# A two-layer convolution and attention trunk in split fp32: the second embedding's place, the query plan of the attention loop, softmax sums, squares and a bias

## The chip, the cores and the metric

The kernel runs on one core of a Trainium2 chip. A core has the engines TensorE (PE; matrix products, with PEld for its weight loads), VectorE (DVE), ScalarE (ACT), GpSimd (POOL) and SyncE (SP, which issues most transfers), an on-chip memory SBUF, and PSUM banks in which TensorE leaves its products. Transfers run on 16 DMA engines. The metric is device microseconds of one execution; less is better.

## The reference, cut to what matters

The input is one sequence of 1024 tokens of width 1024, all in fp32. There are two layers. They differ in the mixer; what stands behind it is the same:

```python
# layer 0: causal Conformer convolution
h = x @ w_in + b_in;  a, gate = split(h);  h = a * sigmoid(gate)
h = depthwise_conv(h, w_dw, 31 taps, causal) + b_dw
y = silu(layer_norm(h)) @ w_out + b_out
# layer 1: attention over the last 128 positions; 16 query heads, 4 key/value heads of 64
k, v = rope(x @ w_k), x @ w_v                       # 16 of the 64 dimensions are rotated
scores = where(0 <= qpos - kpos < 128, q @ k.T / 8, -inf)
lse = logaddexp(logsumexp(scores), sink)            # one sink per head
y = (exp(scores - lse) @ v) @ w_o
# both layers i
x = layer_norm(ALPHA * x + y)                       # ALPHA = 4 ** 0.25
x = layer_norm(ALPHA * x + square(relu(x @ w_up)) @ w_down)     # width 4096
x = x + (p[i] @ w_proj) * sigmoid(x @ w_gate)       # p[i]: 1024 x 256
```

The product `p[i] @ w_proj` depends on nothing that the layer computes. It is called the embedding here.

## The kernel before

**Arithmetic.** TensorE multiplies fp32 numbers in a rounded form (fp32r). So each operand is kept as a high part and a low part (the rest), and each product is three matmuls: high x high, high x low, low x high (`mm3`). In the names, `wh` and `wl` are the parts of a weight tile of 128 x 1024, and `xTh` and `xTl` those of the transposed tokens. ScalarE makes the high part by a copy with rounding ("CAST"), and VectorE the low part by a subtraction. A matmul is 128 x 128 weights against up to 512 columns.

**Order.** No engine's program is written out by hand. `Recorder` records every operation in program order; `schedule` is a list scheduler that then places them on the engines by the durations in `cost` and by priority, which is the place in program order plus what `later(by)` adds. It also hands out buffers: each tag (`SLOTS`) has a number of buffers, and an operation waits for a free one. `nc.move(a, b)` makes a buffer of one tag one of another. `nc.after(mark)` lets an operation wait for another one. Since all instructions are issued from one place, they all carry one line: L455 before the change, L467 after it. They are told apart by buffer names, such as ps (PSUM bank), z, g, t (128 x 512 in SBUF), E, X, A, B (larger tiles). `Stream` (`ws`) feeds weights through five slots: a transfer into `raw`, the cast to `wh`, the subtraction to `wl`.

**Stages around the change.**

*Convolution* (`conv`, to about 260 us). `conv_in` makes the gated input of one channel block in four parts, and `taps` does the 31 taps of a block as matmuls, after a trip of the block through HBM (`scr`). The two run interleaved, the taps five steps (LAG) behind, so that the last steps of the loop `for n in range(32 + LAG)` are taps alone. Then come: the embedding of layer 0 (`embed(0, (0, 1), "g")`, 16 output tiles of 6 matmuls, each copied by ScalarE into a buffer g and stored to HBM); the layer norm and SiLU of the convolution in four pairs of token tiles (`conv_ln`); loads of the residual x into the tiles E (tokens 0 to 3) and B (4 to 7), to each half of which VectorE adds the bias `bo`, not before `marks[3]`, the last pair of `conv_ln`; and `mix_out`, the output projection, whose PSUM result VectorE adds to these tiles, followed by a layer norm with a scaling on GpSimd.

*MLP* (`mlp(i)`). 32 blocks of 128 hidden channels. The first `HEAD[i]` (4 in layer 0, 6 in layer 1) and the last two are computed plainly. The others go in pairs with seven products of half size in place of eight, for which `token_forms` must first combine the tokens on VectorE. `square` is the activation, on every PSUM result:

```python
nc.scalar.activation(r, src, AF.Relu)
sq = r if src.buf.space == "PSUM" else src
nc.vector.scalar_tensor_tensor(out=sq, in0=src, scalar=0.0, in1=r, op0=ALU.max, op1=ALU.mult)
```

*Attention* (`attention`, the loop from 1181.9 to 1394.6 us). Keys, the first queries and two value tiles come first. The loop then goes over two pairs of key heads (`gp`) and eight token tiles (`n`); each step has, for two key heads, the `scores` of four query heads (matmuls, ScalarE's copy, VectorE's masked copy, its negated maximum, four exponentials on ScalarE, VectorE's sum and reciprocal, four scalings on GpSimd) and, one step later, the products with the `values`. Beside them TensorE gets filler through `beside(gp, n)`: in the first pair the second token half of the first queries (n = 0 to 2), six value tiles, the later queries (`rest(1, ...)`, n = 3 to 5, both halves) and at n = 7 the embedding of layer 1 through buffers B; in the second pair the output projection's weights at n = 1 and its first two pairs of tiles at n = 2 and 4. The queries go to HBM (qdh, qdl) and come back for the scores into X. Behind the loop stands the rest of the output projection.

Of the kernel before, what the change touches and what calls it, by code (L numbers as in the profile page):

```python
# [16 lines left out]
P = 128  # L17
# [3 lines left out]
NT = T // P  # L21
# [38 lines left out]
HEAD, TAIL = (4, 6), 2  # L60
# [3 lines left out]
WARM = 7  # L64
CST = 256 + NT * 32 + 2 * NH
# [122 lines left out]
class Recorder:  # L188
# [90 lines left out]
    def cost(self, o, outs, allv):  # L279
# [6 lines left out]
        if n == "dma_start":  # L286
            return 380.0
# [19 lines left out]
    def schedule(self):  # L307
# [11 lines left out]
        def both(o):  # L319
            if o.eng == "gpsimd":  # L320
                return o.name != "memset" and o.outv[0].n > 8
# [166 lines left out]
class Emit:  # L488
# [179 lines left out]
    def conv(self):  # L668
# [155 lines left out]
        outs = (x for c in range(8) for x in taps(c))  # L824
        for n in range(32 + LAG):
            next(ins, None)
            if n >= LAG:
                next(outs, None)
        for g in (ins, outs):
            assert next(g, LAG) == LAG  # L830
# [5 lines left out]
        with nc.later(EMBED_BY):  # L836
            self.embed(0, (0, 1), "g")
# [16 lines left out]
    def embed(self, i, cols, tag):  # L854

# [4 lines left out]
        for q, w in zip(cols, wk):  # L860
            for t in range(NT):
# [9 lines left out]
                nc.sync.dma_start(self.proj[i][t][:, q * HT : (q + 1) * HT], sb)  # L871
        ws.done(len(us))
# [146 lines left out]
    def mlp(self, i):  # L1019
# [9 lines left out]
        us = ws.get(4)  # L1029
# [3 lines left out]
        ws.done(4)  # L1033
# [374 lines left out]
    def attention(self):  # L1408
# [12 lines left out]
        ws.add(*[unit[k] for k in range(2, 8)])  # L1421
        us = ws.get(4)
# [26 lines left out]
        for t in range(2):  # L1449
            value_rows(t)  # L1450
# [5 lines left out]
        def beside(gp, n):  # L1456
            if gp == 0:
                if n < 3:
                    rest(0, n, (1,))
                if n % 2 == 0 and n < 6:  # L1460
                    value_rows(n + 2)
                    value_rows(n + 3)
                    if n == 4:
                        ws.done(2)
                if 3 <= n < 6:
                    rest(1, n - 3, (0, 1))
# [3 lines left out]
                return  # L1470
            if n == 1:
                ws.add(*[d["w_o"][0, u] for u in range(4)])
                self.ou = ws.get(4)
            if n in (2, 4):
                self.out_tiles(0, PAIRS[n // 2 - 1], self.ou)
# [50 lines left out]
    def scores(self, n, g, q, keys):  # L1526
# [220 lines left out]
```

## Time and profile before

| | |
|---|---|
| median of three runs | 2173.28 us (2170.75 to 2178.07) |
| the profiled execution's own time | 2170.38 us |
| its span in the trace | 2168.7 us |
| mean granted TensorE clock | 0.998 |
| instructions of TensorE / VectorE / ScalarE / GpSimd | 10187 / 2480 / 1555 / 432 |
| moved by DMA | 341.52 MB, 157 GB/s over the span |

How to read what follows. A *window* row gives, for a stretch from:to in us, the length, and then for TensorE, its weight loads, VectorE, ScalarE and GpSimd the busy time with the number of instructions; the last three are the granted clock, the busy share of the DMA engines and GB/s. For TensorE the sum of its durations is cut to what it covers, since matmuls are pipelined; a matmul's own duration is longer than the time from its start to the next one's start. A *wait* row reads "engine out <- who released it: us in all, count, longest". A *timeline* row has start, duration, engine, operation, out<-in with sizes, and in brackets the idle time before it and what ended that. A *group* row has the operation with its count, then busy us, mean ns of one, and idle time before with its releaser. A *transfer* row has the count, the KB of each and the median us from issue to landing.

### The profile page before, as it was taken

How to read it: one execution, taken by the hardware profiler on the slowest of the kernel's cores; microseconds unless marked ns; L12 is line 12 of the kernel's file. 1: busy time of each engine (PE TensorE's matmuls, PEld its weight loads, DVE VectorE, ACT ScalarE, POOL GpSimd, SP SyncE). 2: the span in 40 equal slices, each digit the busy share in tenths (PEclk: the TensorE clock that was granted, in tenths of full speed). 3: DMA queues.
4: the chain of work that ended last, by engine and by line, in shares of the span. 5: the costliest groups of instructions: out<-in, count | busy, mean ns of one | idle time of the engine just before them, and what ended most of it. 6: DMA issues, size and time to landing. Idle time of an engine off the chain costs nothing.

```text
span 2168.7 us, 28684 instructions
## 1 busy us (share of the span) xinstructions
PE 2147.9 (99%) x10187; PEld 1788.7 (82%) x10187; DVE 1649.9 (76%) x2480; ACT 893.3 (41%) x1555; POOL 252.6 (12%) x432
## 2 busy tenths in 40 slices
PE   9999999999999999999999999999999999999999
PEld 7888888888888888888888887788888888888887
DVE  7667686987777977889555777899677688878983
ACT  5233342444444333353333666543344433333441
POOL 0000042200000000003101444450000000000040
PEclk9999999999999999999999999999999999999999
DMA  7443632334447755541448689232444596455322
GB/s 230 119 115 87 187 126 81 119 130 157 155 152 268 256 174 175 175 131 36 152 134 227 186 240 269 89 126 78 148 154 160 169 333 206 140 171 177 95 68 102
DMA packets 193360, 341.52 MB, mean 157 GB/s; under 512 B 19392, under 2 KB 88512, under 8 KB 193216
## 3 DMA queue, kind: packets, MB, share of 16 engines
q1 hardware_dynamic: 191920, 338.90, 48.8%
q8 instruction: 80, 1.31, 0.2%
q10 hardware_dynamic: 1296, 0.79, 0.1%
q14 instruction: 64, 0.52, 0.1%
HBM read 235.80 MB, written 103.81 MB: 157 GB/s over the span
## 4 chain that ended last, share of the span: by engine, by line
PE 44%; DVE 3%; DMA 3%; SPq 1%; ACT 1%; issue 1%; POOL 0%; DVEq 0%; ACTq 0%; POOLq 0%
PE ps L455 31%; PE tr L455 13%; SPq L455 1%; DVE xTl L455 1%; DVE A L455 1%; DVE wl L455 0%; DMA B<-xsp 0%; ACT z L455 0%; DVE B L455 0%; DVE sm L455 0%; DMA qdh<-A 0%; DVE t L455 0%; DMA X<-qdh 0%; DMA adl<-t 0%; DMA A<-xsp 0%
## 5 line engine op out<-in xcount | busy, mean ns | idle before, releaser
L455 PE MATMUL ps<-xTl,wh 128*128 128x512 f32 x752 | 295.0, 393 | 0.1
L455 PE MATMUL ps<-xTh,wl 128*128 128x512 f32 x752 | 294.3, 392 | 0.0
L455 PE MATMUL ps<-xTh,wh 128*128 128x512 f32 x752 | 293.0, 391 | 0.2 <-ACT xTh L455 0.2
L455 PE MATMUL ps<-xTl,xTh 128*128 128x512 f32 x636 | 247.4, 389 | 0.0
L455 PE MATMUL ps<-xTh,xTl 128*128 128x512 f32 x636 | 247.4, 389 | 0.0
L455 PE MATMUL ps<-xTh 128*128 128x512 f32 x636 | 247.4, 389 | 0.0
L455 ACT CAST wh<-raw 128x1024 fp32r<-128x1024 f32 (+2 forms) x141 | 132.2, 940 | 245.4 <-PE ps L455 114.7
L455 DVE TENSOR_TENSOR wl<-raw,wh 128x1024 fp32r<-128x1024 f32 (+2 forms) x141 | 156.3, 1109 | 95.0 <-ACT wh L455 93.6
L455 POOL TENSOR_SCALAR sm<-sm 128x1 f32<-128x1 f32 x40 | 14.5, 363 | 1322.2 <-DVE sm L455 1320.7
L455 PEld LDWEIGHTS ps<-xTh,wh 128*128 128x128 f32 x752 | 141.2, 188 | 29.9 <-ACT xTh L455 0.9
L455 PEld LDWEIGHTS ps<-xTh,wl 128*128 128x128 f32 x752 | 141.4, 188 | 28.6
L455 PEld LDWEIGHTS ps<-xTl,wh 128*128 128x128 f32 x752 | 141.2, 188 | 28.3 <-DVE xTl L455 1.0
L455 PE MATMUL ps<-wh,xTh 128*128 128x512 f32 (+1 forms) x408 | 156.8, 384 | 0.3 <-ACT xTh L455 0.3
L455 PE MATMUL ps<-wl,xTh 128*128 128x512 f32 (+1 forms) x408 | 156.6, 384 | 0.0
L455 PE MATMUL ps<-wh,xTl 128*128 128x512 f32 (+1 forms) x408 | 156.5, 384 | 0.0
L455 PEld LDWEIGHTS ps<-xTl,xTh 128*128 128x128 f32 x636 | 119.4, 188 | 24.9
L455 PEld LDWEIGHTS ps<-xTh 128*128 128x128 f32 x636 | 119.4, 188 | 24.7
L455 PEld LDWEIGHTS ps<-xTh,xTl 128*128 128x128 f32 x636 | 119.3, 188 | 24.8
L455 ACT CAST xTh<-wh 128x1024 fp32r<-128x1024 f32 x74 | 77.6, 1049 | 122.6 <-PE ps L455 56.4
L455 ACT CAST wh<-g 128x512 fp32r<-128x512 f32 x100 | 59.8, 620 | 152.3 <-PE ps L455 80.6
L455 DVE TENSOR_TENSOR wl<-g,wh 128x512 fp32r<-128x512 f32 x100 | 66.3, 685 | 72.8 <-ACT wh L455 72.8
L455 DVE TENSOR_TENSOR E<-cst,g 128x1152 fp32r<-128x1152 f32 x64 | 86.1, 1352 | 43.5 <-PE ps L455 42.6
(294 smaller groups left out, 4891.3 us busy)
## 6 DMA issues: line engine op xcount, KB each, us to landing
wh<-hid SPq DMA_DIRECT2D x76, 512.0 KB, 4.0
raw<-in_w_up_dram SPq DMA_DIRECT2D x64, 512.0 KB, 3.5
wl<-in_w_down_dram SPq DMA_DIRECT2D x64, 512.0 KB, 4.6
hid<-zz SPq DMA_DIRECT2D x84, 256.0 KB, 2.9
hid<-t SPq DMA_DIRECT2D x78, 256.0 KB, 2.1
raw<-hid SPq DMA_DIRECT2D x34, 512.0 KB, 3.6
B<-scr SPq DMA_DIRECT2D x32, 256.0 KB, 4.1
t<-proj SPq DMA_DIRECT2D x32, 256.0 KB, 3.4
```

The source lines that it names most:

```text
L455: getattr(getattr(nc, o.eng), o.name)(*a, **k)
```

## The change

It has seven parts.

1. `HEAD` becomes (4, 4): in the second MLP two blocks fewer are computed plainly and one pair more by seven products.
2. The first ten output tiles of layer 0's embedding (two per step, `EARLY`) are emitted in the last five steps of the taps loop, through buffers z; the other six follow behind the loop as before.
3. The bias is added to the residual's tiles by 16 accumulating transfers that GpSimd issues, behind the same mark, in place of 16 VectorE additions.
4. `square` takes ScalarE's Square of the Relu result, in place of VectorE's instruction.
5. `beside` follows a table, `PLAN`. The second token half of the later queries moves into the second pair of key heads (n = 0 to 2; their weights are loaded a second time), two value tiles more stand ahead of the loop and the other four go in pairs to n = 1 and 3, and the output projection's weights and its two pairs of tiles move to n = 3, 3 and 5.
6. The embedding of layer 1 moves out of the loop, behind the first half of the output projection, through buffers t.
7. The sums of the exponentials come from `accum_out` of ScalarE's activations; VectorE's sum goes.

The scheduler's cost of a GpSimd transfer is set to 880 with it. By the programs' order TensorE has 10175 matmuls in place of 10187; VectorE 32 sums and 128 squares fewer; ScalarE 128 activations, 7 casts and 3 copies more; GpSimd 16 transfers more; SyncE 1190 transfers in place of 1187.

```diff
-HEAD, TAIL = (4, 6), 2
+HEAD, TAIL = (4, 4), 2
+EARLY = 2
+PLAN = (
+    {
+        0: [("query", 0, 0, (1,))], 1: [("query", 0, 1, (1,)), ("value", 4), ("value", 5)], 2: [("query", 0, 2, (1,))],
+        3: [("value", 6), ("value", 7)], 4: [("query", 1, 0, (0,))], 5: [("query", 1, 1, (0,))],
+        6: [("query", 1, 2, (0,)), ("load",)],
+    },
+    {
+        0: [("query", 1, 0, (1,))], 1: [("query", 1, 1, (1,))], 2: [("query", 1, 2, (1,))],
+        3: [("weight",), ("out", 0)], 5: [("out", 1)],
+    },
+)
...
+        early = self.embed_tiles(0, (0, 1), "z")
         for n in range(32 + LAG):
             next(ins, None)
             if n >= LAG:
                 next(outs, None)
+            if n >= 32:
+                with nc.later(EMBED_BY):
+                    for k in range(EARLY):
+                        next(early)
...
         with nc.later(EMBED_BY):
-            self.embed(0, (0, 1), "g")
+            for k in early:
+                pass
...
                 with nc.after(marks[MARK[t // 4]]):
-                    nc.vector.tensor_tensor(out=xt[q], in0=xt[q], in1=bo[q], op=ALU.add)
+                    nc.gpsimd.dma_start(xt[q], bo[q], accum_op=ALU.add)
...
         sq = r if src.buf.space == "PSUM" else src
-        nc.vector.scalar_tensor_tensor(out=sq, in0=src, scalar=0.0, in1=r, op0=ALU.max, op1=ALU.mult)
+        nc.scalar.activation(sq, r, AF.Square)
...
         ws.add(*[unit[k] for k in range(2, 8)])
+        ws.add(*[unit[k] for k in range(5, 8)])
...
-        for t in range(2):
+        for t in range(4):
             value_rows(t)
...
         def beside(gp, n):
+            for what, *k in PLAN[gp].get(n, ()):
+                if what == "query":
+                    rest(*k)
+                elif what == "value":
+                    value_rows(*k)
+                    if k[0] == NT - 1:
                         ws.done(2)
-                if n == 7:
-                    self.embed(1, (0, 1), "B")
+                elif what == "load":
                     self.load_residual(range(0, 4))
+                elif what == "weight":
+                    ws.add(*[d["w_o"][0, u] for u in range(4)])
+                    self.ou = ws.get(4)
+                else:
+                    self.out_tiles(0, PAIRS[k[0]], self.ou)
...
         for g in PAIRS[2:]:
             self.out_tiles(0, g, self.ou, last=g is PAIRS[-1])
+        self.embed(1, (0, 1), "t")
...
         for h in range(4):
-            nc.scalar.activation(s[:, h, 0 : P + 1], s[:, h, 0 : P + 1], AF.Exp, bias=nm[:, h : h + 1], scale=1.0)
-        nc.vector.tensor_reduce(out=su, in_=s[:, :, 0 : P + 1], axis=AXIS, op=ALU.add)
+            nc.scalar.activation(s[:, h, 0 : P + 1], s[:, h, 0 : P + 1], AF.Exp, bias=nm[:, h : h + 1], scale=1.0,
+                                 accum_out=su[:, h : h + 1])
```

Here is ScalarE's queue where the convolution ends, before: behind the last four of its transfers to scr come the taps' sums for the transposes (g<-ps with 64x256, the constants cst as bias), the first copy of the embedding (g3_586<-ps0_581) and the copies of the convolution's output into A.

```order
L455 ACTIVATE g3_545_2440<-ps0_546_2450,cst_261_325 64x256
L455 ACTIVATE g3_545_2440<-ps1_548_2479,cst_261_325 64x256 x2
L455 COPY g3_586_2728<-ps0_581_2696 128x512
L455 COPY A1_15_79<-tr1_551_2499 128x64
L455 COPY A3_17_81<-tr1_551_2499 128x64
L455 COPY A5_19_83<-tr1_551_2499 128x64
L455 ACTIVATE g2_562_2582<-ps3_557_2550,cst_261_325 64x256 x2
```

The same place after the change:

```order
L467 ACTIVATE g3_545_2440<-ps0_546_2450,cst_261_325 64x256
L467 COPY z0_49_113<-ps3_557_2550 128x512
L467 ACTIVATE g3_545_2440<-ps1_548_2479,cst_261_325 64x256 x2
L467 COPY z1_50_114<-ps2_561_2577 128x512
L467 COPY z2_51_115<-ps3_581_2703 128x512
L467 COPY z3_52_116<-ps0_582_2706 128x512
L467 COPY A1_15_79<-tr1_551_2499 128x64
```

Four tiles of the embedding (z0 to z3) are copied where one was; the first two were computed in banks 3 and 2, while the banks of the taps' sums are 0 and 1.

GpSimd's queue behind the last scaling of the convolution's layer norm (A7 by the factors in sm6), before: it goes on with the small steps of the first layer norm behind the output projection.

```order
L455 TENSOR_SCALAR A7_21_85<-A7_21_85,sm6_631_2979 128x512
L455 TENSOR_SCALAR sm15_639_3013<-sm9_634_2990 128x1
L455 TENSOR_TENSOR sm15_639_3013<-sm15_639_3013,mhalf_263_327 128x1
L455 TENSOR_SCALAR sm1_644_3030<-sm2_643_3028 128x1
L455 TENSOR_TENSOR sm1_644_3030<-sm1_644_3030,mhalf_263_327 128x1
```

After the change, 16 transfers stand between that scaling and those small steps, first the two halves of E0, then of E1, E2 and E3, then B0 to B7; the last four of them and what follows:

```order
L467 DMA B4_597_2785<-bo0_43_107 128x512
L467 DMA B5_600_2813<-bo1_44_108 128x512
L467 DMA B6_606_2844<-bo0_43_107 128x512
L467 DMA B7_611_2881<-bo1_44_108 128x512
L467 TENSOR_SCALAR sm15_638_3027<-sm9_636_3010 128x1
L467 TENSOR_TENSOR sm15_638_3027<-sm15_638_3027,mhalf_263_327 128x1
L467 TENSOR_SCALAR sm1_642_3042<-sm2_641_3040 128x1
```

The layer norm's first small step (sm15) now stands behind all of them; they add the halves of the bias (bo0, bo1) in place.

TensorE where the second pair of key heads begins, before: matmuls of the embedding (ps0, tr1 <- wh, wl), transposes of probabilities (ident, z), the first scores of the second pair (E2, X0) and products with values (A, bo or v0).

```order
L455 MATMUL ps0_1944_11587<-wl0_1838_11021,wh1_1843_11052 128x512
L455 MATMUL ps5_1912_11422<-ident_262_326,z2_1888_11309 128x128
L455 MATMUL ps0_1944_11587<-wh0_1839_11025,wl4_1842_11049 128x512
L455 MATMUL ps3_1938_11554<-E2_1830_10972,X0_1819_10918 128x128 x4
L455 MATMUL tr0_1943_11584<-E2_1830_10972,X0_1819_10918 128x128 x4
L455 MATMUL ps1_1952_11636<-A8_1906_11391,bo0_1831_10979 128x512
```

After the change:

```order
L467 MATMUL ps2_1955_11589<-xTh_264_328,wh0_1828_10974 128x512
L467 MATMUL ps5_1923_11418<-E2_1821_10945,X0_1807_10864 128x128 x4
L467 MATMUL ps4_1930_11449<-E2_1821_10945,X0_1807_10864 128x128 x4
L467 MATMUL ps2_1955_11589<-xTl_265_329,wh0_1828_10974 128x512
L467 MATMUL ps2_1955_11589<-xTh_264_328,wl1_1829_10979 128x512
```

The embedding's matmuls around these scores have become those of the later queries (ps2 <- xTh or xTl with a query weight), and they go on into the second pair.

More of the change, by code (lines that the diff above doesn't have):

```diff
@@ L286, in cost @@
         if n == "dma_start":
-            return 380.0
+            return 880.0 if e == "gpsimd" else 380.0
         if e == "scalar":
@@ L320, in both @@
             if o.eng == "gpsimd":
-                return o.name != "memset" and o.outv[0].n > 8
+                return o.name not in ("memset", "dma_start") and o.outv[0].n > 8
             if o.eng != "vector":
@@ L854, in embed, with embed_tiles @@
     def embed(self, i, cols, tag):
+        for k in self.embed_tiles(i, cols, tag):
+            pass
+    def embed_tiles(self, i, cols, tag):
         nc, d, ws = self.nc, self.d, self.ws
@@ L871, in embed @@
                 nc.sync.dma_start(self.proj[i][t][:, q * HT : (q + 1) * HT], sb)
+                yield
         ws.done(len(us))
@@ L1027, in mlp @@
         ws.add(*[d["w_up"][i, f] for f in last])
-        us = ws.get(4)
+        us = ws.get(min(HEAD[i], 4))
         for h in range(2):
@@ L1032, in mlp @@
                 self.store(i, f, (f % 2, h), self.up(f, h, us[f]))
-        ws.done(4)
+        ws.done(min(HEAD[i], 4))
         def alone(f):
@@ L1456, in beside @@
         def beside(gp, n):
[L1457 to L1463, printed above, removed]
+            for what, *k in PLAN[gp].get(n, ()):
[4 more added lines that the diff above has]
+                    if k[0] == NT - 1:
                         ws.done(2)
-                if 3 <= n < 6:
-                    rest(1, n - 3, (0, 1))
-                if n == 7:
-                    self.embed(1, (0, 1), "B")
+                elif what == "load":
                     self.load_residual(range(0, 4))
[L1470 to L1475, printed above, removed]
+                elif what == "weight":
[3 more added lines that the diff above has]
+                    self.out_tiles(0, PAIRS[k[0]], self.ou)
         self.x = [None] * NT
```

## The prediction

> **What bounds the kernel now.** I read the page first, then the windows by 50 us, then TensorE's waits, then windows and a timeline of each place where those waits lie.
>
> ```profile
> span 2168.7 us, 28684 instructions
> ...
> PE 2147.9 (99%) x10187; PEld 1788.7 (82%) x10187; DVE 1649.9 (76%) x2480; ACT 893.3 (41%) x1555; POOL 252.6 (12%) x432
> ```
>
> TensorE is busy for 99% of the span, so the change can win only in two ways: fewer matmuls, or less time that TensorE loses between them. The first column of the windows is what TensorE does when nothing holds it, and where something does:
>
> ```profile
> 500.00:550.00 50.00, 50.00 (x222) 41.35 (x221) 34.73 (x53) 21.37 (x35) 0.00 (x0) 1.00 0.45 154
> 1350.00:1400.00 50.00, 49.21 (x251) 39.46 (x250) 44.86 (x96) 33.54 (x92) 26.22 (x56) 1.00 0.35 102
> ```
>
> 222 matmuls of 512 columns in 50 us are 0.225 us each; that is my price of one. In the second row the other engines come near to their limit: VectorE 44.86 of 50 (90%, the highest share outside the forms of the MLP), ScalarE 33.54. TensorE's waits, longest first:
>
> ```profile
> PE ps L455 <- DVE z L455: 3.3, 1, 3.3
> PE ps L455 <- DMA X<-qdl: 2.8, 1, 2.8
> PE ps L455 <- DVE g L455: 2.5, 1, 2.5
> PE ps L455 <- POOL z L455: 1.6, 1, 1.6
> PE ps L455 <- ACT t L455: 1.1, 1, 1.1
> ```
>
> The first, second and fourth are in the attention loop, the third and fifth where the convolution ends. The long MLP stretches have none, so an edit there is worth only the matmuls it removes.
>
> **The attention loop** runs from 1181.9 to 1394.6 us; its two halves are the two pairs of key heads.
>
> ```profile
> 1181.90:1290.00 108.10, 106.53 (x612) 91.78 (x613) 76.71 (x159) 68.49 (x183) 43.61 (x99) 0.98 0.72 201
> 1290.00:1394.60 104.60, 100.58 (x515) 81.04 (x515) 88.00 (x192) 73.96 (x200) 55.76 (x125) 0.98 0.69 192
> 1181.90:1394.60 212.70, 207.11 (x1126) 172.82 (x1127) 164.71 (x350) 142.45 (x382) 99.37 (x222) 0.98 0.70 197
> ```
>
> The first half has too much filler, the second too little: there VectorE works 88.0 of 104.6 us and TensorE stands 4 us. The new order has the 96 matmuls of the embedding behind the loop and two value tiles (48 matmuls of 256 columns, at about 0.12 us) ahead of it, and five 512-column matmuls fewer between the first score and the last product with values: 96 x 0.225 + 48 x 0.12 + 5 x 0.225 = 28.5 us that TensorE works elsewhere, at full pace. So the loop **breaks even at 212.7 - 28.5 = 184.2 us**; that is the number to beat.
>
> ```profile
> 1315.53 1.14 PE L455 MATMUL ps<-E,X 128*128 128x256 f32 x4 [3.28 <-DVE z L455]
> 1316.47 0.63 PE L455 MATMUL tr<-wh,xTl 128*128 128x512 f32 x1
> 1316.90 0.63 PE L455 MATMUL tr<-wh,xTh 128*128 128x512 f32 x1
> ...
> 1312.76 1.04 ACT L455 CAST wh<-raw 128x1024 fp32r<-128x1024 f32 x1 [3.84 <-DMA raw<-in_w_o_dram]
> ...
> 1281.00:1316.00 35.00, 31.48 (x163) 25.56 (x162) 22.62 (x50) 25.65 (x65) 14.02 (x33) 1.00 0.96 276
> ```
>
> These rows (TensorE's and ScalarE's timelines, then a window) explain the longest wait. ScalarE stood 3.84 us for the first weights of the output projection, with the copies of the next scores queued behind it; the weights were late because the 16 DMA engines were 96% busy from 1281 to 1316, when the embedding's 16 stores of 256 KB joined the loads of keys and queries. In the new order neither stores nor embedding are there. That wait goes, and with it the slow matmuls behind it: starts 0.43 us apart (1316.47, 1316.90) for some seven matmuls, 1.5 us. Gain 4.8 us. Of the 1.6 us on "POOL z" (the scaled probabilities) I count the whole, as the chain of a softmax loses a VectorE step:
>
> ```profile
> L455 DVE TENSOR_REDUCE sm<-z 128x4 f32<-128x516 f32 x64 | 43.2, 682 | 1.8 <-ACT z L455 1.0
> L455 ACT ACTIVATE z<-z,sm 128x129 f32<-128x129 f32 x128 | 47.0, 401 | 5.4 <-DVE sm L455 4.9
> L455 ACT CAST v<-g 128x128 fp32r<-128x128 f32 x5 | 1.4, 285 | 0.0
> ```
>
> 32 of the 64 reductions go: 32 x 0.68 = 21.8 us off VectorE. In their place 128 exponentials carry an accumulator, which no row shows. Its bounds are nothing and a whole second instruction of 0.40 us; I take 0.1, the 401 - 285 of an activation with a per-partition operand over the plain instruction of the same width, since the accumulator is one such operand more. That is 128 x 0.1 = 13 us on ScalarE. It sheds 16 copies of the embedding, two value copies and one weight cast, 11.4 us by the mean of these groups. So at 184 us ScalarE would be busy 142.5 - 11.4 + 13 = 144 us (78%, now 67%), VectorE 164.7 - 21.8 - 2.5 = 140 us (76%, now 77%): no engine near the 90% seen above, and both halves alike. For the thinner filler I give 1.4 us back. **Loop: -5.0 us.** The 2.8 us on X<-qdl stays, because the loads wait for the queries' trip through HBM and the first scores move by only 0.5 us (two value tiles more ahead, one query block less).
>
> Behind the loop one more wait goes, as the embedding's 96 matmuls stand there and need nothing of the attention: **-0.8 us.**
>
> ```profile
> 1398.99 0.50 PE L455 MATMUL tr<-wh,xTh 128*128 128x512 f32 x1 [0.79 <-ACT xTh L455]
> ```
>
> **Where the convolution ends**, ScalarE's queue holds TensorE up:
>
> ```profile
> 245.80 1.60 PE L455 MATMUL ps<-B,E 128*128 128x256 f32 x12
> 249.92 0.47 PE L455 MATMUL ps<-wh,wh 128*128 128x512 f32 x1 [2.51 <-DVE g L455]
> ...
> 250.69 0.61 PE L455 MATMUL ps<-wh,wh 128*128 128x512 f32 x1
> ...
> 254.16 0.60 PE L455 MATMUL tr<-ident,g 128*128 128x128 f32 x4
> ...
> 246.45 2.08 ACTq L455 DMA_DIRECT2D scr<-zz  x4
> ```
>
> The embedding's first tile takes the PSUM bank that the taps have just left, and that bank waits for four DMA issues on ScalarE (2.08 us) and the sums behind them. Then eight matmuls from 250.69 to 254.16 start 0.43 us apart (3.47 / 8). In the new order the first two tiles sit in banks freed earlier, so TensorE has 12 matmuls (2.7 us) to do in just that gap, and stays at full clock: 2.5 + 8 x 0.2 = 4.1 us. I take **-4.0 us**; the layer norm's chain behind has less filler left, but the output projection's matmuls now stand there instead. The Trainium skill's page "TensorE: Matmul & The Clock Gate" (Part 1: The HAM clock gate) says that the clock halves after an idle window of about 3.4 us; here 2.51 us of waiting was enough, so this trace does not bear the length out, which a window that runs freely may explain. By that page only the wait would count: -2.5 us.
>
> **The bias.** Sixteen VectorE additions become accumulating DMAs on GpSimd.
>
> ```profile
> 306.78 4.90 DVE L455 TENSOR_TENSOR E<-E,bo 128x512 f32<-128x512 f32 x8
> 311.59 4.90 DVE L455 TENSOR_TENSOR B<-B,bo 128x512 f32<-128x512 f32 x8
> 316.41 2.47 DVE L455 SCALAR_TENSOR_TENSOR E<-E,ps 128x512 f32<-128x512 f32 x4
> ...
> hid<-t SPq DMA_DIRECT2D x78, 256.0 KB, 2.1
> B<-scr SPq DMA_DIRECT2D x32, 256.0 KB, 4.1
> ```
>
> VectorE's 9.8 us lie beside matmuls and gain nothing. The DMAs wait for the same mark, about 303 us in the new order, and the first four output tiles are done near 310; the next tiles need the banks of tiles 0, 1, 2, so transfers 1, 3 and 5, at 310, 311 and 313. No row shows a DMA from GpSimd. Per transfer in line: at least 0.52 us (the 2.08 us of four issues above), at most the 4.1 us of the slowest landing of this size. Fifth at 305.6 or at 323.5; nothing lost, or 10.5 us plus some 2 of slow clock. I stay near the 2.1 us of the nearest row, a store out of SBUF: fifth at 313.5. **+1.0 us.** Queued behind the sixteen on GpSimd is the first layer norm's scale, wanted at 348. The Trainium skill's page "DMA: Bandwidth & Descriptors" (Anatomy of one DMA — SWDGE) gives 2.0 us plus bytes / 436e3 for such a DMA, an estimate of 2.6 us for 256 KB; one after another that would put the fifth at 316 and cost 3 us. No run here shows it yet.
>
> **The second MLP's head.** Two pairs of blocks computed plainly become one pair more of the seven-product kind: 96 matmuls become 84, 12 x 0.225 = 2.7 us. But the combined tokens must be ready 22 us earlier.
>
> ```profile
> 1461.70:1497.00 35.30, 35.30 (x159) 29.31 (x158) 34.57 (x56) 14.43 (x24) 0.00 (x0) 1.00 0.31 104
> 1497.00:1519.00 22.00, 22.00 (x99) 18.23 (x98) 18.13 (x28) 7.39 (x13) 0.00 (x0) 1.00 0.24 69
> 405.00:440.00 35.00, 35.00 (x156) 29.00 (x155) 34.80 (x57) 15.45 (x27) 0.00 (x0) 1.00 0.22 74
> ```
>
> They are wanted at about 1497 instead of 1519, and VectorE is full until then (34.57 of 35.30). The third row is the first MLP, which has this head already: VectorE as full, TensorE without a gap. The squares leave VectorE too, here some nine of 0.68 us. **-2.2 us**, 0.5 kept for a late form.
>
> **The squares** otherwise cost nothing:
>
> ```profile
> L455 ACT ACTIVATE z<-t 128x512 f32<-128x512 f32 x21 | 13.3, 634 | 0.0
> L455 DVE SCALAR_TENSOR_TENSOR t<-t,z 128x512 f32<-128x512 f32 x21 | 14.4, 684 | 0.0
> ```
>
> 128 of them move; some 12 per 50 us at 0.63 raise ScalarE from 21.4 to 29 of 50 us (row 500:550). If that cover went, each would cost its 0.63.
>
> **The sum**: -5.0 - 0.8 - 4.0 + 1.0 - 2.2 = -11.0 us. The profiled execution took 2170.38 us, 1.7 more than its span: 2159.4. The median of the runs, 2173.28, lies 2.9 above it, so a median comes to **2162 us**.
>
> **Rivals.** (1) *ScalarE becomes the loop's bound*: the accumulator costs a second instruction, 0.40 us. ScalarE then works 142.5 - 11.4 + 51.3 = 182 us; at the 90% an engine reaches here the loop takes 203, 18.5 over break-even, and the other terms (-6) leave 2173.3 + 12.5 = 2186, slower. It decides from 0.36 us each (177 / 0.9 = 196.7). For it: 128 of them in strict order before each reciprocal. Against: the operand rows above. (2) *The bias transfers run one by one* at 4.1 us: the sum is -11 - 1 + 12.5, 2174, no change. (3) *The loop only breaks even*: the waits come back elsewhere, since 28 us of filler left: -6, 2167, at the edge. For it: the start's wait stays and the second half's VectorE chain is only a seventh shorter.
>
> **How the numbers follow.** About 0.3% (6.5 us) is what a measurement tells from no change: 2166.8 to 2179.8. Forecast 0.58, all of it faster; (2) and (3) together 0.24, taken as no change; (1) and a loop slower by more than its gain for other reasons 0.18, slower. At best all of the loop's listed waits and both slow stretches go (some 15 us more with the bounds at zero): 2147. The top takes in most of (1): 2184.
>
> **What would show it.** Right: no wait on "DVE g" near 250 us and granted clock 1.00 there; loop under 184 us with ScalarE near 78%; no wait of TensorE behind E or B tiles from 305 to 325; 12 matmuls fewer. Wrong: exponentials far over 0.5 us, DMA rows on GpSimd over 2 us apart with TensorE waiting for "DVE E", or a wait before the first matmul on X near 1497.

## The result, and the profile after

The changed kernel takes 2170.3 us in the median of 14 runs (2166.13 to 2176.1), the kernel before 2173.53 (14 runs, 2170.75 to 2178.07). The ratio is 0.9986 with a 95% interval of 0.9977 to 0.9995: 3.2 us less, where 11 were forecast (2162). The profiled execution took 2166.13 us, the lowest of the 14, so its trace flatters the change: it is 4.3 us shorter than that of the kernel before.

The page's first lines after the change show the matmuls that went and the work that moved from VectorE to ScalarE:

```profile
span 2164.4 us, 28692 instructions
...
PE 2144.2 (99%) x10175; PEld 1783.9 (82%) x10175; DVE 1556.6 (72%) x2319; ACT 984.8 (45%) x1821; POOL 266.1 (12%) x447
```

ScalarE has 266 instructions more, not the 138 of the program's order. The other 128 are in the next view, the groups of ScalarE in the loop: a read of the accumulator behind each exponential.

```profile
L467 ACT ACTIVATE z<-z,sm 128x129 f32<-128x129 f32 x128 | 51.2, 402 | 8.4 <-DVE sm L467 8.0
L467 ACT ACTIVATION_READ_ACCUMULATOR z<-z,sm 128x1 f32 x128 | 24.2, 189 | 0.0
```

TensorE's waits after the change, longest first:

```profile
PE ps L467 <- DMA X<-qdl: 4.4, 3, 2.3
PE tr L467 <- DVE t L467: 1.7, 2, 1.5
PE ps L467 <- DVE t L467: 1.5, 1, 1.5
PE ps L467 <- DMA B<-scr: 1.4, 1, 1.4
PE tr L467 <- ACT z L467: 1.3, 1, 1.3
PE tr L467 <- POOL A L467: 1.2, 2, 0.9
```

The waits that the prediction named are gone: "DVE g" (2.5), "DVE z" (3.3), "POOL z" (1.6) and "ACT xTh" behind the loop (0.8). In their place stand others. "DMA X<-qdl", the queries on their way back from HBM, comes three times where it came once; "DMA B<-scr" and "POOL A" are where the convolution ends.

The loop, from the first score to the last product with values, and the two halves of it (columns as before):

```profile
1181.30:1283.10 101.80, 96.40 (x543) 80.73 (x543) 74.13 (x156) 75.13 (x249) 51.71 (x110) 0.98 0.77 207
1283.10:1366.80 83.70, 82.10 (x434) 65.49 (x435) 69.93 (x158) 65.33 (x240) 46.56 (x111) 1.00 0.60 160
1181.30:1366.80 185.50, 178.50 (x977) 146.23 (x978) 144.06 (x313) 140.46 (x488) 98.27 (x221) 0.99 0.69 186
```

The loop takes 185.5 us; 184.2 was break-even and 179.2 the forecast, 5.0 below it. VectorE's 144 us and ScalarE's 140 are near the forecast's 140 and 144. Neither is near its limit, and TensorE still stands 7.0 us, against 5.6 in the longer loop before. So the gain outside the loop arrived in this trace, nearly whole, and the loop lost 1.3 us where 5.0 were to be won.

The next rows are the start of the second pair of key heads, on TensorE and then on SyncE:

```profile
1283.12 1.11 PE L467 MATMUL ps<-E,X 128*128 128x128 f32 x8 [0.83 <-DMA X<-qdl]
```

```profile
1264.27 0.48 SPq L467 DMA_DIRECT2D qdl<-A  x1
...
1270.79 5.22 SPq L467 DMA_DIRECT2D X<-qdh  x8
...
1278.39 1.26 SPq L467 DMA_DIRECT2D X<-qdl  x2
```

SyncE issues one of these loads every 0.65 us (5.22 / 8), and here takes the high parts of all eight tiles before the first low part. The first tile's low part goes out 7.6 us after its high part, and the scores need both. A like order (seven, four, eight and eight high parts before the first low one) stands ahead of all four first scores after a trip of queries: 2.31 us (1181.3), 1.25 (1226.4), 0.83 (1283.1), and 1.04 (1323.3, put down to "issue"). Theory Q was that these four waits ate the loop's gain. Its rivals were the accumulators on ScalarE (A) and the thinner filler (F), the filler being the matmuls that TensorE can do while a softmax is under way.

### The profile page after: what moved, and what is told of

The parts are those of the page before. It is cut to its first block, busy times and chain, and to the rows that moved or that the text cites. A ratio compares the mean times of both kernels' runs of the same rounds, so it can differ in the third digit from the quotient of the medians.

```text
span 2164.4 us, 28692 instructions
## 1 busy us (share of the span) xinstructions
PE 2144.2 (99%) x10175; PEld 1783.9 (82%) x10175; DVE 1556.6 (72%) x2319; ACT 984.8 (45%) x1821; POOL 266.1 (12%) x447
## 4 chain that ended last, share of the span: by engine, by line
PE 47%; DVE 2%; DMA 2%; ACT 1%; SPq 1%; issue 0%; POOL 0%; DVEq 0%; ACTq 0%
PE ps L467 32%; PE tr L467 14%; SPq L467 1%; ACT z L467 1%; DMA qdh<-A 1%; DVE z L467 1%; DMA X<-qdl 0%; DVE sm L467 0%; DVE A L467 0%; DVE xTl L467 0%; POOL sm L467 0%; DMA X<-qdh 0%; DVE t L467 0%; DMA raw<-in_w_o_dram 0%; POOL A L467 0%
## 5 line engine op out<-in xcount | busy, mean ns | idle before, releaser
L467 PE MATMUL ps<-xTl,wh 128*128 128x512 f32 x720 | 283.1, 394 | 0.2 <-DVE xTl L467 0.2
L467 PE MATMUL ps<-xTh,wh 128*128 128x512 f32 x720 | 281.4, 392 | 0.4 <-ACT xTh L467 0.4
L467 PE MATMUL ps<-xTh,wl 128*128 128x512 f32 x720 | 281.8, 392 | 0.0
L467 PEld LDWEIGHTS ps<-xTh,wh 128*128 128x128 f32 x720 | 135.5, 188 | 29.4 <-ACT xTh L467 1.3
L467 PEld LDWEIGHTS ps<-xTl,wh 128*128 128x128 f32 x720 | 135.4, 188 | 27.1 <-DVE xTl L467 1.4
L467 PEld LDWEIGHTS ps<-xTh,wl 128*128 128x128 f32 x720 | 135.3, 188 | 27.0
```

Source lines behind the costliest of these rows:

```text
L467: getattr(getattr(nc, o.eng), o.name)(*a, **k)
```

## The experiments

All ratios are to the kernel before, with 95% intervals. Two of them are told apart when they differ by more than about 0.0013 (0.0018 for the runs with fewer repeats); 0.001 is 2.2 us.

**e1: queries' loads in turn.** Only the planner's order of the loads into X changes:

```diff
             self.nc.sync.dma_start(dst, src)
+        hi, lo = self.nc.ops[-2:]
+        hi.deps.update((x, True) for x in lo.deps if x.name == "dma_start" and x is not hi)
         return q
...
                 r = end + delay(o, x) + (0.0 if o.eng in ("tensor", "alloc") else x.slack)
+                if o.eng == x.eng == "sync" and o.outv[0].buf is x.outv[0].buf and o.outv[0].buf.tag == "X":
+                    r = free["sync"]
```

> The changed kernel, except that the loads of the queries into X come in turn (high and low part of one tile, then of the next) in place of all eight high parts ahead of the low ones. In the changed kernel's trace SyncE issues these loads about 0.65 us apart, so the low part of the first tile is issued some 4 to 5 us after its high part, and TensorE stands before the first scores at four places: 2.3 + 1.25 + 0.83 us on X<-qdl and 1.04 us put down to issue. Theory Q (these four waits are what the shorter loop pays: the queries' trip through HBM is now bare at four places, before at one): the four waits fall to under 1 us in all, the loop from 185.5 to about 181, the whole by 4 us. Theory A (the accumulators load ScalarE) and theory F (a softmax chain with too little filler beside it is late wherever it stands): the waits move to other tiles, the loop stays within 1.5 us of 185.5.

Measured: 2163.71 us, 0.9964 (0.9952 to 0.9977), 4.8 us less than the changed kernel. TensorE's waits of this run:

```profile
PE tr L469 <- POOL A L469: 5.6, 3, 3.1
PE ps L469 <- ACT z L469: 1.8, 1, 1.8
PE ps L469 <- DVE t L469: 1.5, 1, 1.5
```

All four waits for queries are gone from the list, and part of them came back as 3.1 us on GpSimd's masked probabilities (A) and 1.8 us on z. Ahead of the former GpSimd itself stood 5.14 us until a store (adl<-t) had landed. The loop is 183.4 us, not the 181 that theory Q expected, and starts 3.0 us sooner. In all the turn was worth what theory Q said, 4 us. Whether they are what ate the forecast is another question; e9 answers it.

**e2: sums back on VectorE, new plan.**

```diff
-AF.Exp, bias=nm[:, h : h + 1], scale=1.0, accum_out=su[:, h : h + 1])
+AF.Exp, bias=nm[:, h : h + 1], scale=1.0)
+        nc.vector.tensor_reduce(out=su, in_=s[:, :, 0 : P + 1], axis=AXIS, op=ALU.add)
```

> The changed kernel with the sums of the exponentials back on VectorE (32 reductions), without accumulators. In the changed kernel each of the 128 exponentials is followed by an instruction of 0.189 us that reads the accumulator, 24.2 us of ScalarE in the loop. Theory A (this is what the loop lost): ScalarE's busy time in the loop falls by 24 us, the waits on ACT z and DVE t (1.3 and 1.5 us) go, the whole is 3 us faster than the changed kernel. Theory Q: the waits for the queries stay, the whole stays within 1 us. If the accumulators help as the prediction had it (a shorter chain), it is 1 to 2 us slower, with waits on POOL z.

Measured: 2170.93 us, 0.9994 (0.9985 to 1.0003). It isn't faster, so theory A fails in the new plan. It is 1.7 us slower, within the noise, and its trace has 2.1 us on "POOL z" that the changed kernel's has not, as the third expectation had it.

**e3: embedding back in the loop.** `self.embed(1, (0, 1), "B")` at n = 7 of the first pair in place of the call behind the loop. The stream hands out weights in the order in which they were added, so here the embedding and the later queries multiply by one another's weights; number and size of all work stay the same.

> The changed kernel with the second embedding back at the last step of the first pair of key heads (buffers B), so 96 matmuls, 21.6 us, are filler again; the break-even of the loop is then 184.2 + 21.6 = 205.8 us. Theory F: with the filler back the waits of the first pair and at its end go, the loop comes 3 us under break-even or better, the whole 3 to 4 us faster than the changed kernel. Theory Q: the wait at the start of the second pair (0.83) goes, the others stay; the 16 stores share the queue with the loads again, so the whole is within 1.5 us of the changed kernel. Theory A: within 1.5 us.

Measured: 2170.61 us, 0.9987 (0.9976 to 0.9999), like the changed kernel. With the filler back TensorE still waited 2.95 us at the first scores, 1.63 and 1.3 us on z and 2.06 us on the later queries: theory F fails here.

**e4: old plan with accumulators, e5: old plan with VectorE's sums.** The table holds the old order, two value tiles ahead of the loop, no second load of weights, the embedding in the loop; e5 has e2's edit as well.

```diff
+        0: [("query", 0, 0, (1,)), ("value", 2), ("value", 3)], 1: [("query", 0, 1, (1,))],
+        2: [("query", 0, 2, (1,)), ("value", 4), ("value", 5)], 3: [("query", 1, 0, (0, 1))],
+        4: [("value", 6), ("value", 7), ("query", 1, 1, (0, 1))], 5: [("query", 1, 2, (0, 1))],
+        7: [("embed",), ("load",)],
...
+    {1: [("weight",)], 2: [("out", 0)], 4: [("out", 1)]},
```

> The changed kernel with the whole attention plan of before (queries, values, weights, embedding in the loop; no second load of weights), but with the accumulators and all other parts of the change. It tells what the accumulators alone did in the old order, and what the new plan did. Theory Q: one trip (2.7 us at the first scores) is bare as before, the mid trips are covered; with the accumulators the wait of 3.3 us for the output projection's weights stays, so the loop is 212 +- 1.5 us and the whole within 1.5 us of the changed kernel. Theory A: 24 us more of ScalarE in the second pair, where it was busy 74 of 104.6: the loop is 215 us or more, the whole slower than the changed kernel by 3 us.

> The changed kernel with the old attention plan and with the sums back on VectorE: of the change only the early embedding, the bias by transfers, the squares on ScalarE and the second MLP's head remain. With the changed kernel (new plan, accumulators: 0.9986 of before), the run with the new plan and VectorE's sums (0.9994) and the one with the old plan and accumulators (1.0009) it closes a square of four. If plan and accumulators act apart (additive), this one stands at 0.9994 + 1.0009 - 0.9986 = 1.0017 of before, slower than all. If the accumulators only harm in the old plan (theory A holds there: three waits on ScalarE, 7.5 us, in that run's loop), it is the old loop with the gains outside it, 4 to 5 us faster than before, 0.998.

Measured: e4 2175.81 us, 1.0009 (1.0 to 1.0018); e5 2169.26 us, 0.9981 (0.9971 to 0.9991). The four are not additive. e5 is the old loop with all of the change outside it, 4.1 us faster than before (2.0 to 6.3). It is level with the whole change (0.9986): the attention part is worth nothing that can be told. The accumulators cost 6 us in the old plan; in e4's trace, of the slowest of its eleven runs, waits for ScalarE's copies stand on top:

```profile
PE ps L465 <- ACT A L465: 6.1, 2, 3.3
PE ps L465 <- DMA X<-qdl: 3.6, 1, 3.6
```

**e6: first embedding late, e7: bias on VectorE, e8: squares' second step on VectorE.** Each undoes that part alone, by its lines of the change.

> The changed kernel without the early tiles: the whole first embedding behind the loop over the taps, through g, as before. In the changed kernel's trace the wait of 2.51 us for the bank and the slow matmuls behind it are gone, but TensorE waits 1.41 us for the last block's load from scr at 255.8 and 0.81 + 0.94 us for the scaled tiles of the convolution's layer norm at 289 and 292. Prediction: this kernel is 4.0 us slower than the changed one. What the changed trace says: 2.4 us slower at most, since the waits on scr and on GpSimd go again; with them gone, 0.5 to 2.5 us slower.

> The changed kernel with the bias added by 16 VectorE instructions, as before. Prediction: 1.0 us faster than the changed kernel; rival of transfers one by one: 12 us faster. The changed kernel's trace has no wait of TensorE between 300 and 350 us behind a tile E or B: no difference, within 1 us.

> The changed kernel with the second step of the squares back on VectorE. Prediction: nothing, within 1 us; at the head of the second MLP, where VectorE combines the tokens, up to 1 us slower than the changed kernel, with a wait on xTl or the combined tokens near 1480 to 1500.

Measured: e6 2171.93 us, 0.9991 (0.9983 to 1.0); e7 2172.11, 0.9993 (0.9985 to 1.0002); e8 2170.75, 0.9982 (0.9973 to 0.9991). None is told apart from the changed kernel; e6 is slower by 1.1 us with an interval that holds nothing as well as 3. In e6's trace the wait of 2.67 us on "DVE g" at 250 is back.

e8 has the same order of instructions in the loop as the changed kernel (only PSUM banks have other tags), yet its loop took 195.5 us in the profiled execution against 185.5. (The order is that of e6 and e7 too, with loops of 190.2 and 189.4 us, so 185.5 is the best of four.) The windows of e8, around two waits and over the loop, show why:

```profile
1178.00:1187.00 9.00, 7.61 (x28) 6.79 (x29) 3.08 (x6) 1.98 (x8) 0.00 (x0) 0.62 0.51 132
1288.00:1296.00 8.00, 7.49 (x27) 6.53 (x28) 3.34 (x7) 1.81 (x6) 0.46 (x1) 0.57 0.85 212
1179.40:1374.90 195.50, 185.16 (x978) 151.83 (x979) 144.22 (x313) 140.83 (x488) 96.21 (x221) 0.96 0.65 177
```

The granted clock is 0.62 and 0.57 there; in the changed kernel's trace it is 1.00 in both windows. More on this below.

**e9: the kernel before with loads in turn, e10: e5 with loads in turn, e11: e1 with the embedding in the loop** (its weights now in the right place of the stream).

> The kernel before with the alternating loads of the queries alone. Its trace has one bare trip, 2.75 us on X<-qdl at the first scores with half a clock for some 3.4 us behind it. Theory Q (the new plan laid four trips bare, and that is what its gain paid): the alternation gains less here than in the changed kernel, 2 to 3.5 us, ratio 0.9985 to 0.999. If it gains as much as there (4.8 us, ratio 0.9978), the bare trips are no property of the new plan.

> The run with the old plan and VectorE's sums (0.9981 of before) with the alternating loads added. Theory Q: one bare trip (3.8 us in that run's trace) goes; ratio 0.9965 to 0.997. Against the changed kernel with alternating loads (0.9964) it tells what plan, embedding and accumulators are worth once the trips are covered: by the prediction's sum 5.8 us, so this run would stand at 0.9964 + 0.0027 = 0.9991; by theory Q half of it at least, 0.9978; if the two come out equal, the attention part of the change is worth nothing even then.

> The changed kernel with alternating loads and with the second embedding back in the loop, at the last step of the first pair, its weights ahead of the second load of the queries' weights in the stream. Theory F (too little filler): the waits that are left with alternating loads, 3.15 us on POOL A and 1.78 us on ACT z, go, and it is 3 us or more faster than with alternating loads alone (0.9964), at 0.995. Against it: the earlier run with the embedding in the loop lost as much as the changed kernel; then within 1.5 us of 0.9964.

Measured: e9 2168.43 us, 0.9982 (0.9974 to 0.9991); e10 2165.05, 0.9968 (0.9956 to 0.998); e11 2166.75, 0.9972 (0.9961 to 0.9983). The turn gains 3.9 us in the kernel before, 2.8 in e5 and 4.8 in the changed one; these are not told apart, and 3.9 lies between theory Q's 3.5 and the 4.8 against it. What decides is that e10 is level with e1 (0.9964): with the trips covered in both, the attention part is still worth nothing that can be told. So theory Q falls as the reason. F fails again with e11.

**e12: transfers nearer their measured cost.** The planner reckons 0.38 us for an issue and at least 2.8 us from issue to landing. The traces show 0.60 to 0.65 us for issues into X and E, and median landings of 4.0 to 4.6 us for most loads (many stores land in 2.0 to 3.2). e12 is e1 with this:

```diff
-            return 880.0 if e == "gpsimd" else 380.0
+            return 880.0 if e == "gpsimd" else 620.0 if isinstance(outs[0], View) and outs[0].buf.tag in ("X", "E") else 380.0
...
-                finish(o, max(dma, t + 2800.0))
+                finish(o, max(dma, t + 4200.0))
```

> The changed kernel with alternating loads, and with the scheduler's costs of transfers near those of the trace: 620 for an issue into X or E (0.60 to 0.65 us in the trace) in place of 380, and 4200 from issue to landing (medians of 4.0 to 4.6 us) in place of 2800. If the waits that are left stand where the planner thinks a transfer lands earlier than it does (the last block's load from scr, 0.8 to 2.7 us at 256 us; tiles behind late loads), it is 2 to 4 us faster than with alternating loads alone. If they are the chain of softmax, within 1.5 us.

Measured: 2155.76 us (2155.06 to 2156.55), **0.9922** (0.9909 to 0.9935): 16.8 us faster than before, 8 to 9 beyond e1 (by the medians and by the ratios). Waits of this run, longest first, and then windows of the loop and of the convolution's end:

```profile
PE ps L469 <- DVE t L469: 3.3, 3, 1.6
PE ps L469 <- POOL B L469: 0.9, 1, 0.9
PE tr L469 <- DVE A L469: 0.9, 1, 0.9
PE ps L469 <- DMA X<-qdl: 0.8, 1, 0.8
```

```profile
1174.50:1354.40 179.90, 174.58 (x968) 142.02 (x967) 145.12 (x315) 140.00 (x488) 101.60 (x220) 1.00 0.70 196
250.00:300.00 50.00, 49.56 (x281) 41.86 (x280) 35.48 (x74) 28.71 (x64) 27.15 (x35) 1.00 0.75 242
```

Between 250 and 300 us TensorE stands 0.4 us; in the changed kernel 3.2:

```profile
250.00:300.00 50.00, 46.84 (x270) 39.63 (x269) 38.91 (x78) 31.52 (x68) 28.56 (x35) 1.00 0.73 237
```

The wait on scr there is gone, and how can be read off the two timelines: the changed kernel had done its early tiles by 253.8 and stood until the block from scr was there, at 255.8; e12 kept ten of the embedding's matmuls for that time (253.5 to 255.9). TensorE's rows, first of the changed kernel, then of e12:

```profile
253.78 0.60 PE L467 MATMUL tr<-ident,g 128*128 128x128 f32 x4
255.79 6.48 PE L467 MATMUL ps<-B,E 128*128 128x256 f32 x52 [1.41 <-DMA B<-scr]
...
253.51 0.49 PE L469 MATMUL ps<-wh,wh 128*128 128x512 f32 x1
...
255.68 0.40 PE L469 MATMUL ps<-wh,wh 128*128 128x512 f32 x1
255.94 6.25 PE L469 MATMUL ps<-B,E 128*128 128x256 f32 x50
```

The filler was there all along; the planner had spent it before the moment at which it was needed. That the other waits went for the same reason was not followed one by one, and the two numbers were not tried apart. No stretch at half clock is left in the loop (1.00), and the four runs lie within 1.5 us of each other, where the changed kernel's fourteen spread over 10.

**e13 to e18** put the same costs under other orders: the kernel before with loads in turn (e13); e10 (e14); the changed kernel without the loads in turn (e15); e12 with VectorE's sums (e16); e14 with accumulators (e17); e11 (e18).

> The kernel before with alternating loads and the transfer costs near the trace's. Theory P (the gain that was forecast for the change, 11 us or 0.0051, was eaten because the planner lets TensorE's filler run out ahead of landings that come later than it thinks; with true costs the change is worth what was forecast): this stands at 0.9922 + 0.0051 = 0.997. Rival G (true costs give the same to any order, and the change is worth its measured 3 us with them too): 0.9922 + 0.0014 = 0.9936.

> The changed kernel with the old attention plan, embedding in the loop and VectorE's sums, with alternating loads and transfer costs near the trace's. Against 0.9922 it gives the worth of the attention part under true costs. Theory P: the forecast 5.8 us, so 0.9949. Rival G: within 1.5 us, 0.9915 to 0.993.

> The changed kernel with the transfer costs near the trace's, without the change that lets the two loads of a tile go in turn. If the order of the loads was the matter, it stays near the changed kernel (0.9986) plus what the costs gave beside alternation (8 us, 0.0037): 0.995. If the landing times are the whole matter, the waits for queries go without alternation too: 0.9925 or less.

> The changed kernel with alternating loads, transfer costs near the trace's, and VectorE's sums in place of the accumulators. In the changed trace an exponential with its read of the accumulator starts 0.398 us after the one before it, against 0.304 without, so the accumulators cost ScalarE 12 us and save VectorE 22. If that is a gain in the loop, this run is 1 to 3 us slower than 0.9922: 0.993 to 0.9935; if plan and accumulators depend on one another by chance of the order only, within 1.5 us of 0.9922.

> The old plan with the embedding in the loop, and the accumulators, with alternating loads and transfer costs near the trace's: the fourth corner beside 0.9922 (new plan, accumulators), 0.9948 (new plan, VectorE's sums) and 0.9928 (old plan, VectorE's sums). If the accumulators are worth 5 us in any plan, 0.990 and the fastest of all; the new plan is then a loss of 4 us. If the new plan needs them and the old one does not (as with the planner's own costs, where they cost 6 us in the old plan), 0.9928 or slower.

> The changed kernel with the embedding back in the loop, alternating loads and transfer costs near the trace's. If the embedding's 96 matmuls are better used as filler in the loop (theory F under true costs), 0.991 or less; if they only make room for as much loss elsewhere, within 1.5 us of 0.9922; if the stores and their buffers hurt, slower than 0.993.

| planner with measured transfer costs | median us | ratio (95%) |
|---|---|---|
| e12 whole change | 2155.76 | 0.9922 (0.9909 to 0.9935) |
| e18 embedding in the loop | 2157.19 | 0.9925 (0.9912 to 0.9939) |
| e14 old plan, VectorE's sums | 2157.04 | 0.9928 (0.9916 to 0.9941) |
| e17 old plan, accumulators | 2159.41 | 0.9932 (0.992 to 0.9945) |
| e15 whole change, loads not in turn | 2159.08 | 0.9938 (0.9926 to 0.9951) |
| e16 new plan, VectorE's sums | 2161.34 | 0.9948 (0.9934 to 0.9962) |
| e13 kernel before | 2163.11 | 0.9956 (0.9942 to 0.9969) |

The whole change is worth 7.4 us here (e13 to e12), more than its 3.2 with the planner's own costs, less than the 11 forecast. Of it 6.1 us come from the parts outside the attention (e13 to e14) and 1.3 us, not told apart from nothing, from the attention (e14 to e12). So rival G holds for the attention. The rest comes to the 6.0 that the prediction's sum had for it, but theory P, which wanted 11 in all, does not hold as it stood. The accumulators are worth 5.6 us in the new plan (e16 to e12), and nothing that can be told in the old one (e14 to e17). What they relieve is seen in e16's waits, where the scaled probabilities stand on top:

```profile
PE ps L469 <- POOL z L469: 4.5, 5, 2.0
PE ps L469 <- DVE t L469: 4.0, 3, 1.5
```

In e12 the wait on POOL z is 0.6 us. Without accumulators the new plan is 4.3 us slower than the old (e14 to e16), just beyond the noise. The likely reason, by these waits, is that it takes away the filler that hid the chain of a softmax, and that the accumulators then shorten the chain by about as much.

The turn of the loads is worth 3.5 us with these costs, within the noise (e15 to e12), and e15's waits on X<-qdl come to 0.5 us without it: with later landings in the plan the trips are covered in either order. In the five orders that were measured with both sets of costs, the new costs gain 5.7 to 10.4 us.

## Why the prediction was right or wrong, point by point

- **The loop, -5.0 us: wrong, and this is the step that failed.** Break-even (184.2) was right: the loop took 185.5 with the matmuls as counted, and the first scores moved by 0.6 us. The two waits that it counted as gain (3.28 us behind the late weights, 1.57 on "POOL z") went as described. What failed is the price of what would come in their place, "For the thinner filler I give 1.4 us back", for which it had no row. The new order had five others of 0.8 to 1.5 us, 5.9 us in all, and a stretch at half clock behind one of them (1.7 us): two more trips on X<-qdl, one put down to "issue", one on z and one on t. The traces fall 6.7 us short of the sum (4.3 in place of 11.0), and the loop is 6.3 of it. This was the third rival, "the waits come back elsewhere". By e5 and by e14 the attention part is worth nothing that can be told under either set of costs.
- **The wait at the start, "stays": right** (2.75 to 2.31 us). That the same trip would become bare again for each half of the later queries was not seen, though the diff splits it.
- **Accumulators, 0.1 us each: right in size, wrong in form.** They are a second instruction of 0.189 us, but it overlaps: two exponentials in a row start 0.304 us apart before; after, the read starts 0.305 us behind the exponential and the next exponential 0.093 behind the read (medians), so 0.094 more. The first rival, 0.40 each and a loop of 203 us, did not come. Busy time (51.2 + 24.2 us) overstates the cost.
- **Behind the loop, -0.8: right.** No wait of TensorE follows the last product with values.
- **Convolution end, -4.0 with +1.0 for the bias: the mechanism right, the size too large.** The 2.51 us and the half clock went. In their place came 1.41 us for the last block's load from scr, and 0.81 + 0.94 us for the scaled tiles of the layer norm, which has less filler before it; 1.1 us on t went. In the two traces TensorE's spacing beyond its median (the time from each matmul to the next, over the median of the same pair of shapes) sums from 200 to 350 us to 8.7 before and 6.2 after: -2.4 in place of -3.0. With the transfer costs of e12 the same place falls to 3.1. The run that undoes the early tiles alone (e6) tells 1.1 us for them, not apart from nothing.
- **Bias, +1.0: mis-sized; it is 0 within the noise.** The transfers landed 4.8 us (E) and 5.8 us (B) after issue in the median, but most landed 1.3 to 1.9 us apart; the first three were issued from 297.05 on, ahead of the 303 reckoned, and the fifth landed at 307.5, not 313.5. No wait on E or B follows, and e7 is not told apart from the changed kernel. The estimate from the Trainium skill's page "DMA: Bandwidth & Descriptors" (Anatomy of one DMA — SWDGE), 2.6 us for each and one after another, is too short for one transfer here and too long for a row of them. The second rival, 4.1 us each in line, did not come.
- **The second MLP's head, -2.2: right.** 12 matmuls fewer, TensorE busy for all of 1470 to 1497 with VectorE at 26.88 of 27.00. No run undoes this part alone.
- **Squares, 0: right**, by e8 within the noise.

The prediction's parts outside the loop sum to -6.0; e5 measures -4.1 for them (-2.0 to -6.3), e10 against e9 -3.0, and e14 against e13 -6.1. The time lies inside the range, but that range was 37 us wide; it is near the third rival's 2167.

## What to carry to other kernels

When a change removes a wait from a busy stage, ask what would end last there next, and price the moved work at break-even until a view shows otherwise; a wait is a place where filler ran out, not a fixed cost. In a statically planned kernel compare the planner's constants with the trace first: two numbers for issue and landing were worth 6 to 10 us, more than the seven edits. And test edits in pairs: here the accumulators cost 6 us in the old plan with the planner's own costs, and gained 5.6 in the new plan with the measured ones.

## What the runs showed of the hardware that was not expected

The granted clock halves in stretches of 3.41 us or 6.83 us, which cost TensorE about 1.7 or 3.4 us of work. In the trace before they stand behind waits of 2.51, 2.75 and 3.28 us. But 2.31 us at 1181.3 brought none in the changed kernel, while 2.65 us at the same place in e8 brought 6.8, and 1.51 us with 0.28 behind it brought a stretch of 3.4 at 1272.6. So the same order of the loop loses 1.7 us of clock in one execution and 8.5 in another (half of 6.8, 3.4 and 6.8), and in the 14 runs of the changed kernel the lowest mean clocks (0.996) go with the longest times (2174.81 and 2176.1 us).

The Trainium skill's page "TensorE: Matmul & The Clock Gate" (Part 1: The HAM clock gate) has the gate judge by a free-running window of 3413 ns. The traces agree with the window: within each execution the stretches begin a whole number of 3.41 us apart. But the page's rule of a whole idle window is not borne out: part of one is enough. The rows show such windows, the first four of the changed kernel, the last two of e8:

```profile
1177.00:1180.41 3.41, 1.97 (x17) 1.77 (x15) 0.16 (x1) 1.38 (x2) 0.00 (x0) 1.00 1.09 211
1180.41:1183.82 3.41, 2.54 (x19) 2.39 (x19) 1.80 (x4) 0.50 (x2) 0.00 (x0) 1.00 0.88 198
1269.17:1272.58 3.41, 1.63 (x6) 0.97 (x6) 2.61 (x6) 1.79 (x9) 1.62 (x4) 1.00 0.92 291
1272.58:1275.99 3.41, 3.41 (x11) 2.40 (x10) 2.39 (x5) 1.84 (x5) 3.11 (x6) 0.50 0.80 188
...
1175.82:1179.23 3.41, 0.92 (x8) 0.72 (x6) 0.00 (x0) 1.66 (x2) 0.00 (x0) 1.00 0.83 208
1179.23:1186.06 6.83, 6.67 (x24) 6.03 (x25) 3.08 (x6) 0.59 (x3) 0.00 (x0) 0.50 0.45 116
```

The edge at 1180.41 cuts the wait of 2.31 us into 1.44 and 0.87, and the clock stays; e8's wait lies in one window with 2.49 us of standing, and the two waits at 1272 share one with 1.78. Over the 20 traces, without the ends of the program, all 30 windows at full clock in which TensorE stood 1.9 us or more were followed by half clock, 11 of the 23 with 1.45 to 1.9, and none with less. So whether a wait of 2 to 3 us costs clock depends on how an edge happens to cut it. No run moved a wait against the windows on purpose, and why some stretches last two windows stays open.
